# Loading the first tile of a split GELU-multiply with one transfer instead of two

## The chip, the cores and the metric

The kernel runs on one core of a Trainium2 chip. The metric is the device time of one execution in microseconds (us); less is better. Before the change the median of three runs is 469.26 us (469.21 to 469.45).

A core has computing engines with their own instruction streams (of these the kernel uses VectorE, called DVE in the profile, and ScalarE, called ACT), a SyncE (SP) that here only issues transfers, and 16 DMA engines that move the data between the device memory (HBM) and the on-chip buffers. Engines wait for each other and for transfers with semaphores.

## The reference

The input x is 32 x 512 x 2048 in float32. The last dimension is cut in two halves; the exact GELU of the first half is multiplied with the second.

```python
half_dim = x.shape[-1] // 2
x1, x2 = x[..., :half_dim], x[..., half_dim:]
gelu_x1 = 0.5 * x1 * (1 + erf(x1 / np.sqrt(2)))
return (gelu_x1 * x2).astype(np.float32)
```

The input has 134.22 MB and the output 67.11 MB. Every byte is read or written once.

## The kernel before

The 16384 rows are cut into 16 tiles of 1024 rows. A tile lies on 128 partitions, with R = 8 consecutive rows of 2048 numbers on each, so a partition's part of a tile is one contiguous stretch of 64 KB in HBM on the way in and 32 KB on the way out. There are two input buffers and two output buffers; tile i uses buffer k = i % 2 of each.

Everything is ordered by hand, with semaphores and three instruction streams:

- SP issues the loads (`load`, line 46) into queue q1. Loads 0 and 1 go out at the start (lines 60 to 64), load 0 in two halves: rows 0 to 3 of each partition with the semaphore `first[0]`, rows 4 to 7 with `first[1]`. Load i+2 goes out when the last multiplication of tile i is done (lines 107 to 109), since it overwrites the buffer that this reads.
- ACT computes the GELU (line 81) from the input buffer into the output buffer, and DVE multiplies it in place with the second half of the input rows (line 89). Both work in steps: rows 0 to 4 and 5 to 7 in most tiles; 0 to 1, 2 to 3 and 4 to 7 in tiles 0 and 15 (`pieces`, lines 72 and 73).
- ACT also issues the stores of tiles 0 to 13 (`store`, line 51) into queue q10. A store waits for the multiplication, and whatever comes next in ACT's program stands behind this wait. Tile 0 is stored in two halves of four rows, the first between ACT's second and third step. The store of tile 14 and the two half stores of tile 15 are issued by SP, into q1.

ACT begins a tile when its semaphore `ready[k]` has reached the count of everything issued on it so far (line 79). On `ready[k]` both the loads into buffer k and the stores from buffer k are counted, 16 each:

```python
            if i == 0 and lo % 4 == 0:
                nc.scalar.wait_ge(first[lo // 4], 16)
            elif lo == 0:
                nc.scalar.wait_ge(ready[k], n[ready[k].name])
```

So tile i (from 2 on) begins when both load i and store i-2 have landed; the second is needed because the GELU overwrites the output buffer. Only tile 0 waits for its two half loads apart, the second one ahead of the step of rows 4 to 7.

Of the kernel before, what the change touches and what calls it, by code (L numbers as in the profile page):

```python
# [1 line left out]

# [4 lines left out]

GELU = mybir.ActivationFunctionType.Gelu


@with_exitstack
def kernel(
    ctx: ExitStack,
    tc: tile.TileContext,
    x: bass.AP,
    out: bass.AP,
):
    nc = tc.nc
    P = nc.NUM_PARTITIONS

    x_flat = x.flatten_outer_dims()
    out_flat = out.flatten_outer_dims()
    n_rows, dim = x_flat.shape
    half = dim // 2

    R = 8
    x_t = x_flat.rearrange("(n p r) d -> n p r d", p=P, r=R)
    o_t = out_flat.rearrange("(n p r) d -> n p r d", p=P, r=R)
    n_tiles = x_t.shape[0]
    x_bufs = [nc.alloc_sbuf_tensor(f"x{k}_tile", [P, R, dim], x.dtype) for k in range(2)]  # L30
    o_bufs = [nc.alloc_sbuf_tensor(f"o{k}_tile", [P, R, half], out.dtype) for k in range(2)]

    first = [nc.alloc_semaphore(f"first{j}") for j in range(2)]
    ready = [nc.alloc_semaphore(f"ready{k}") for k in range(2)]
    gelu_done = nc.alloc_semaphore("gelu_done")
    mul_done = nc.alloc_semaphore("mul_done")
    tail_stored = nc.alloc_semaphore("tail_stored")
    n = {sem.name: 0 for sem in [*first, *ready, gelu_done, mul_done, tail_stored]}  # L40

    def counted(ins, sem, by):
        ins.then_inc(sem, by)
        n[sem.name] += by

    def load(i, rows, sem):
        ins = nc.sync.dma_start(out=x_bufs[i % 2][:, rows, :], in_=x_t[i][:, rows, :])  # L47
        counted(ins, sem, 16)
        return ins

    def store(queue, i, rows, sem):
        queue.wait_ge(mul_done, n[mul_done.name])
        counted(
            queue.dma_start(out=o_t[i][:, rows, :], in_=o_bufs[i % 2][:, rows, :]), sem, 16
        )

    for ins in (  # L60
        load(0, slice(0, 4), first[0]),
        load(0, slice(4, 8), first[1]),
        load(1, slice(0, 8), ready[1]),
    ):
        tc.no_tile_sem_insts.add(ins.ins.name)
    tc.close()
    tc.compile()  # L67

    for i in range(n_tiles):
        k = i % 2  # L70
        last = i == n_tiles - 1
        pieces = i == 0 or last
        steps = ((0, 2), (2, 4), (4, 8)) if pieces else ((0, 5), (5, 8))
        for lo, hi in steps:
            rows = slice(lo, hi)
            if i == 0 and lo % 4 == 0:
                nc.scalar.wait_ge(first[lo // 4], 16)
            elif lo == 0:
                nc.scalar.wait_ge(ready[k], n[ready[k].name])
            counted(  # L80
                nc.scalar.activation(  # L81
                    out=o_bufs[k][:, rows, :], in_=x_bufs[k][:, rows, :half], func=GELU
                ),
                gelu_done,
                1,
            )
            nc.vector.wait_ge(gelu_done, n[gelu_done.name])
            counted(
                nc.vector.tensor_mul(  # L89
                    out=o_bufs[k][:, rows, :],  # L90
                    in0=o_bufs[k][:, rows, :],
                    in1=x_bufs[k][:, rows, half:],
                ),
                mul_done,
                1,
            )
            if pieces and hi % 4 == 0:
                if last:
                    store(nc.sync, i, slice(hi - 4, hi), tail_stored)
                else:  # L100
                    store(nc.scalar, i, slice(hi - 4, hi), ready[k])
        if not pieces:
            if i == n_tiles - 2:
                store(nc.sync, i, slice(0, R), tail_stored)
            else:
                store(nc.scalar, i, slice(0, R), ready[k])
        if i + 2 < n_tiles:
            nc.sync.wait_ge(mul_done, n[mul_done.name])
            load(i + 2, slice(0, R), ready[k])


    nc.scalar.drain()  # L112
    for sem in (*first, *ready):
        nc.scalar.sem_clear(sem)
    nc.vector.drain()
    nc.vector.sem_clear(gelu_done)
    nc.sync.sem_clear(mul_done)
    nc.sync.wait_ge(tail_stored, n[tail_stored.name]).then_inc(
        tail_stored, -n[tail_stored.name]
    )  # L120


# [1 line left out]
_INS = ['x']  # L124
_OUTS = [((32, 512, 1024), 'float32')]


# [23 lines left out]
```

## Time and profile before

| | us |
|---|---|
| median of the runs | 469.26 |
| span of the profiled execution, first to last instruction | 467.9 |
| median less span | 1.4 |
| DVE busy, 34 multiplications | 140.5 |
| ACT busy, 35 instructions | 115.5 |
| DVE idle, waiting for ACT | 319.7 |
| ACT idle, waiting for stores | 301.6 |
| ACT idle, waiting for loads | 35.7 |
| one tile in the steady state (start of ACT to start of ACT) | 29.0 |

The page gives the span of the profiled execution and no total for it; what lies around the span is seen only by setting it beside the median of the runs.

How it is read: the page shows the busy time of each engine, the use of the DMA engines in 40 slices of 11.7 us, and the two queues with their packets, megabytes and share of the time of the 16 engines. The waits name the engine that waited, the tensor that it was going to write, and what released it ("<-"), with the sum, the number of times and the longest. The timeline has start, duration, engine, line, operation and shapes; "ACTq" and "SPq" are the issues of transfers. A transfer has landed when the instruction that waits for it starts.

Across the whole execution the 16 tiles' 134.22 MB were read and 67.11 MB written, 430 GB/s over the span.

### The profile page before, as it was taken

To read this page: it belongs to the slowest core of one execution; us is meant where nothing else is said; L and a number is where in the kernel's file an instruction comes from. 1 tells how busy PE (TensorE), PEld (TensorE's weight loads), DVE (VectorE), ACT (ScalarE), POOL (GpSimd) and SP (SyncE) were. 2 spreads that over 40 slices of the span, in tenths; PEclk is the share of its full clock that TensorE was granted. 3 is DMA by queue.
4 is the path that set the end of the run, shared out by engine and by line. 5 is a ranking of instruction groups with operands and counts; after the bars stand their busy time and mean duration, and the time that the engine had idled before them with its cause. 6 is when DMAs were issued, how large, how long until landed. Compare 5 with 4: busy or idle time off the path is not lost.

```text
span 467.9 us, 152 instructions
## 1 busy us (share of the span) xinstructions
DVE 140.5 (30%) x34; ACT 115.5 (25%) x35; POOL 0.2 (0%) x4
## 2 busy tenths in 40 slices
DVE  0330514207052060511606116060150702507043
ACT  1320606042060410604106050050500506014060
POOL 0000000000000000000000000000000000000000
DMA  8999999999999999999999999999999999999998
GB/s 359 448 448 443 403 405 492 409 403 448 459 437 403 434 417 493 403 403 448 476 420 403 445 406 493 403 406 445 487 409 403 445 451 448 403 434 417 493 389 373
DMA packets 5041, 201.34 MB, mean 430 GB/s; under 512 B 560, under 2 KB 560, under 8 KB 560
## 3 DMA queue, kind: packets, MB, share of 16 engines
q1 hardware_dynamic: 2880, 142.61, 70.6%
q10 hardware_dynamic: 2160, 58.72, 29.1%
q14 instruction: 1, 0.01, 0.0%
HBM read 134.22 MB, written 67.11 MB: 430 GB/s over the span
## 4 chain that ended last, share of the span: by engine, by line
DMA 76%; DVE 14%; ACT 8%; ACTq 0%; SPq 0%; issue 0%
DMA out_dram<-o_tile 66%; DVE o_tile L89 14%; DMA x_tile<-in_x_dram 10%; ACT o_tile L81 8%; ACTq L112 0%; SPq L47 0%
## 5 line engine op out<-in xcount | busy, mean ns | idle before, releaser
L89 DVE TENSOR_TENSOR o_tile<-o_tile,x_tile 128x5120 f32<-128x5120 f32 (+3 forms) x34 | 140.5, 4171 | 319.7 <-ACT o_tile L81 319.7
L81 ACT ACTIVATE o_tile<-x_tile 128x5120 f32<-128x5120 f32 (+3 forms) x34 | 114.3, 3407 | 337.4 <-DMA out_dram<-o_tile 301.6
L81 ACT ACT_TABLE_LOAD x1 | 1.3, 1283 | 2.9 <-PEq L67 2.9
L135 POOL MEMSET const-bfloat16-1.0<- 128x1 bf16 x1 | 0.1, 101 | 0.0
L135 POOL MEMSET const-uint8-127<- 128x1 uint8 x1 | 0.1, 101 | 0.0
L135 POOL MEMSET const-float32-0.0<- 128x1 f32 x1 | 0.1, 98 | 0.2 <-issue 0.2
L135 POOL MEMSET const-float32-1.0<- 128x1 f32 x1 | 0.1, 98 | 0.0
## 6 DMA issues: line engine op xcount, KB each, us to landing
out_dram<-o_tile ACTq DMA_DIRECT2D x13, 4096.0 KB, 44.7
x_tile<-in_x_dram SPq DMA_DIRECT2D x2, 4096.0 KB, 16.6
out_dram<-o_tile ACTq DMA_DIRECT2D x2, 2048.0 KB, 34.5
out_dram<-o_tile SPq DMA_DIRECT2D x1, 4096.0 KB, 25.2
out_dram<-o_tile SPq DMA_DIRECT2D x2, 2048.0 KB, 7.8
x_tile<-in_x_dram SPq DMA_DIRECT2D x15, 44.2
```

The costliest lines, as they stand in the source:

```text
L81: nc.scalar.activation(out=o_bufs[k][:, rows, :], in_=x_bufs[k][:, rows, :half], func=GELU),
L89: nc.vector.tensor_mul(out=o_bufs[k][:, rows, :], in0=o_bufs[k][:, rows, :], in1=x_bufs[k][:, rows, half:],),
L135: nc = _bacc.Bacc("TRN2", target_bir_lowering=False, num_devices=1)
```

## The change

The two half loads of tile 0 become one load of all eight rows of each partition. It is counted on `ready[0]`, like the later loads of that buffer; the two `first` semaphores go, and with them the wait ahead of rows 4 to 7 of tile 0. The steps of tile 0 (rows 0 to 1, 2 to 3, 4 to 7) and its two half stores stay as they are.

```diff
-    first = [nc.alloc_semaphore(f"first{j}") for j in range(2)]
     ready = [nc.alloc_semaphore(f"ready{k}") for k in range(2)]
@@
     for ins in (
-        load(0, slice(0, 4), first[0]),
-        load(0, slice(4, 8), first[1]),
+        load(0, slice(0, 8), ready[0]),
         load(1, slice(0, 8), ready[1]),
     ):
@@
-            if i == 0 and lo % 4 == 0:
-                nc.scalar.wait_ge(first[lo // 4], 16)
-            elif lo == 0:
+            if lo == 0:
                 nc.scalar.wait_ge(ready[k], n[ready[k].name])
@@
     nc.scalar.drain()
-    for sem in (*first, *ready):
+    for sem in ready:
         nc.scalar.sem_clear(sem)
```

The instructions of ACT and DVE are the same and in the same order; SP issues one transfer fewer.

More of the change, by code (lines that the diff above doesn't have):

```diff
@@ L39 @@
     tail_stored = nc.alloc_semaphore("tail_stored")
-    n = {sem.name: 0 for sem in [*first, *ready, gelu_done, mul_done, tail_stored]}
+    n = {sem.name: 0 for sem in [*ready, gelu_done, mul_done, tail_stored]}
     def counted(ins, sem, by):
```

## The prediction

> **What bounds the kernel now.** I read the page from the top: busy times, the DMA row of the 40 slices, the queues.
>
> ```profile
> span 467.9 us, 152 instructions
> DVE 140.5 (30%) x34; ACT 115.5 (25%) x35; POOL 0.2 (0%) x4
> DMA  8999999999999999999999999999999999999998
> q1 hardware_dynamic: 2880, 142.61, 70.6%
> q10 hardware_dynamic: 2160, 58.72, 29.1%
> ```
>
> The two computing engines are idle most of the time; the queues q1 (all loads and the last three stores, issued by SP) and q10 (the other stores, issued by ACT) keep the 16 DMA engines busy for 70.6 + 29.1 = 99.7% of the span. The kernel is bound by moving 201.34 MB. No order of transfers can gain much: only 0.3% (1.4 us) of the span is not DMA time, and the first packet is in the records only at 1.74 us, after a first issue at 0.73. What a change can do is to open a hole in the DMA.
>
> Then the waits, which show what a tile waits for, and the timeline of both ends.
>
> ```profile
> ACT o_tile L81 <- DMA out_dram<-o_tile: 301.6, 14, 21.9
> ACT o_tile L81 <- DMA x_tile<-in_x_dram: 35.7, 3, 21.1
> ```
>
> ```profile
> 12.76 3.71 ACT L81 ACTIVATE o_tile<-x_tile 128x2048 f32<-128x2048 f32 x2 [8.62 <-DMA x_tile<-in_x_dram]
> 19.23 0.38 ACTq L54 DMA_DIRECT2D out_dram<-o_tile  x1
> 22.46 3.62 ACT L81 ACTIVATE o_tile<-x_tile 128x4096 f32<-128x4096 f32 x1 [5.99 <-DMA x_tile<-in_x_dram]
> 30.57 0.36 ACTq L54 DMA_DIRECT2D out_dram<-o_tile  x1
> 47.20 7.12 ACT L81 ACTIVATE o_tile<-x_tile 128x5120 f32<-128x5120 f32 x2 [21.12 <-DMA x_tile<-in_x_dram]
> 71.57 7.12 ACT L81 ACTIVATE o_tile<-x_tile 128x5120 f32<-128x5120 f32 x2 [17.24 <-DMA out_dram<-o_tile]
> ...
> 432.86 27.74 SPq L54 DMA_DIRECT2D out_dram<-o_tile  x3
> 448.56 7.21 ACT L81 ACTIVATE o_tile<-x_tile 128x2048 f32<-128x2048 f32 x3 [21.87 <-DMA out_dram<-o_tile]
> ```
>
> Fourteen tiles (2 to 15) wait for a store, and not for their load alone: a buffer's semaphore counts the load of tile i+2 and the store of tile i together, and ACT waits for the sum. So a late store holds a tile whose data are there. How stores and loads share the engines stands in the DMA view, cut to the stretches 19 to 24.3, 24.3 to 46.3 and 46.7 to 71 us (packets, MB, share).
>
> ```profile
> q1 hardware_dynamic: 64, 2.10, 96.8%
> ...
> q1 hardware_dynamic: 113, 7.34, 77.4%
> q10 hardware_dynamic: 128, 2.10, 22.2%
> ...
> q1 hardware_dynamic: 144, 8.39, 79.7%
> q10 hardware_dynamic: 144, 2.10, 20.2%
> ```
>
> A transfer is 8 packets on each of 16 engines (one per partition) and a small one for the semaphore: 9 x 16 = 144. While both queues have work the engines take turns, one packet of each, whatever their sizes: in the last stretch all of load 2 (8.39 MB) went with all of the second half store (2.10 MB). The first stretch has no packet of q10, although the first half store was issued at 19.23. Its 64 packets of q1 are 16 semaphores and three data packets per engine; the store's first packet comes at 24.38, 5.15 us after its issue.
>
> Prices of a packet, from landings (starts of ACT). Load packet l (64 KB): half a load took 22.46 - 12.76 = 9.70, so l = 9.70/4 = 2.42. Load packet with a half-store packet (16 KB): 71.57 - 47.20 = 24.37, over 8 is 3.05. With a full store's packet s (32 KB): the next landing is at 100.56, 28.99 later, over 8 is 3.62; so s = 1.20 and the half-store packet is 0.63.
>
> **The change, part by part.**
>
> *One issue less on SP, two semaphores fewer.* SP issues load 1 about 0.43 us earlier (0.38 + 0.05 in the chain). It waits behind load 0 in the same queue until 21.6, so this gives nothing; were that cover gone it would be worth 0.43. At the end ACT clears two semaphores fewer, while SP still waits for the last store (7.2 us in its waits): nothing.
>
> *ACT starts at 22.46 and not at 12.76.* Load 0 has the same bytes on the same queue, so it lands when its second half did. The first half store is issued 19.23 - 12.76 = 6.47 later, at 28.93. ACT's last activation is queued behind it; its issue takes 0.38, and from there the activation, the multiplication and the issue take 30.57 - 22.46 = 8.11: the second half store (ACT) and load 2 (SP, waiting on the same multiplication) go out at 37.4 instead of 30.57. Neither makes the DMA idle: load 1 is queued and lasts past 41.
>
> *What is late next: the stores fall behind the loads.* Before, only one packet of load 1 went ahead of the first half store, so its 8 packets just fitted in with load 1's last seven (113 and 128 packets above), and since then a load and a store always ended together. Now load 1 runs alone from 21.6. If the store again needs 5.15 us, its first packet comes after 28.93 + 5.15 = 34.1, with 5 load packets gone (21.6 + 5 x 2.42 = 33.7). Of the half stores' 16 packets per engine, 4 get a turn before load 1 ends:
> - load 1 lands at 22.46 + 19.4 + 4 x 0.63 + 0.4 (the 0.4 is what the same sum leaves open before, 24.74 - 19.4 - 8 x 0.63 = 0.3, rounded up) = 44.8. Tile 1 takes 60.50 - 47.20 = 13.30 to its store's issue: 58.1 (before 60.50).
> - load 2 lands at 44.8 + 24.4 = 69.2, but 4 half-store packets are left, and tile 2 waits for them: 4 turns with load 3, 69.2 + 4 x 3.05 = 81.4 (before 71.57). Store 2 and load 4 are issued at 94.7 (before 84.86).
> - load 3 lands at 81.4 + 4 x 3.62 = 95.9; its last packet is some 1.0 us earlier, at 94.9. Load 4 needs about 1.0 from issue to first packet (the first load: 0.73 to 1.74), so 95.7: q1 is empty for a moment, and store 1, of which 4 packets are left, runs one or two alone. No DMA time is lost, and the lag shrinks to 3 packets (or 2).
> - With lag r, a load lands r x 1.20 earlier than before and its tile then waits r turns: net r x 2.42 later, 7.3 us for r = 3. Before, load i+2 was issued 15.7 us ahead of load i+1's landing (84.86 to 100.56), 14.7 ahead of its last packet. With lag r it is 14.7 - 3.62r: 3.8 for r = 3, enough against 1.0, and 0.2 for r = 4, not enough. So 3 is the largest lag that keeps itself, and nothing in the steady state (29.0 us per tile) takes it away.
>
> *The end.* Before, the SP queue carries store 14 and the two half stores of tile 15 without a hole: 8.39 MB from 448.56 to 467.9. With r store packets of tile 13 left when load 15 lands, these take turns with store 14's (1.20 each): load 15 lands 1.20r earlier, tile 15 is ready 1.20r later, 3.6 for r = 3. The half stores of tile 15 are issued that much later while the data ahead of them are gone on time, so the queue runs dry. The last half store was issued 27.4 after 432.86, at 460.23, and took 7.6 to land. Alone it would take 2.10 MB at the load rate, 4.85, plus what the first load needs beyond its bytes (12.76 - 0.73 - 9.70 = 2.33): 7.2. So 0.4 us of slack is there, at most 0.9, if the 0.5 us that the first packet of all took longer (1.71 against 1.21) isn't paid by a warm engine. Cost: 1.20r less 0.4 to 0.9, which is 2.7 to 3.2 for r = 3, 1.5 to 2.0 for r = 2, 0.3 to 0.8 for r = 1.
>
> I take r = 3 and 2.8, as the engines are warm at the end. The sum: 467.9 + 2.8 = 470.7 for the span. The page gives no total for its execution; the median of the runs, 469.26, is 1.4 above the span, and I add the same: 472.0 us.
>
> **A rule beside it.** The row first: in the stretch from 24.3 to 46.3 us 128 packets of the store stand among 113 of the load, single turns. The Trainium skill, "DMA: Bandwidth & Descriptors", section "Queues, rings and completion order", has an engine drain a whole packet of some 9 to 17 descriptors of one ring before it switches; a transfer here has 9 per engine, so a store would go as a block after one load. By that rule no store would fall behind by more than its own block, tiles would not wait for turns, and the sum would be 469.3. The row contradicts it, and I go by the row.
>
> **The rivals.**
> - *Not slower: the lag heals (469.3).* The wait of 5.15 us may not be a time but a number of packets already taken. Three per engine stand between the store's issue and its first packet. If three go first again, load packets 4, 5 and 6 (the fourth starts at 28.9), the store comes at 36.2 and only 3 of its packets run with load 1. Then 5 are left when load 2 has landed, load 4 is issued at 97.1, and load 3's last packet ends at 93.7; the 5 store packets of tile 1 need 6.0 us alone, to 99.7, and load 4 comes at about 98. They use the hole up, loads and stores are level again, and all is as before from tile 3 on. It decides if more than 5 load packets go first. For it: the count of three. Against it: 0.36 us stand empty ahead of that first store packet, as if it had just arrived, not long been taken.
> - *A lag of one (470.0).* If load 4's first packet needs nearer 2.5 us than 1.0, three store packets run alone: +0.3 to 0.8. Against it: the last half stores followed each other with no hole, the second 1.8 us after its issue.
> - *A lag of four or more, or holes in the middle (472.9 to 476).* Lag 4 kept costs 3.9 to 4.4. If the whole shift of tile 0 (37.4 - 30.57 = 6.9) came through, 476.2. Against that: full slices of the DMA everywhere.
> - *Faster.* Only the 0.43 us of the issue and the packets' overhead are to be had: 468.8 at best.
>
> **How the numbers follow.** No change is what lies within 0.2% (0.94 us) of 469.26. Lag 3: 0.42; lag 2 (471.0): 0.18; four or more: 0.07; lag 1: 0.07, nearly all within 0.2%; healed: 0.24; faster by over 0.2%: 0.02. Slower is 0.42 + 0.18 + 0.07 + 0.01 = 0.68, same 0.30, faster 0.02. The range takes in the healed case and lag 3 with its upper price: 469.0 to 473.0, which leaves out about 1 in 10. The likeliest case's own range, with lag 2, is 470.7 to 472.5.
>
> **What would show it.** Issues at 28.9 and 37.4; tile 1 starting at 44.8, before its old 47.20, tile 2 at 81.4, tile 3 at 108 and tile 4 at 137 (before 129.57), and then steps of 29 us with tiles 7 us late; the last tile starting at 452.2 and a slice under full DMA at the end. Tile 3 back at about 100 and the last tile at 448.6 would show the healed case. I am wrong if the engines don't take single turns while load 1 is under way, or if the lag drains in the steady state by a way that the trace of before can't show.

## The result, and the profile after

The changed kernel takes 474.13 us (median of four; 471.82 to 474.60) against 469.25 us before: ratio 1.0088, 95% interval 1.0069 to 1.0107. It is slower by 4.9 us, as forecast in sign, but above the range (469.0 to 473.0) and by nearly twice the 2.7 us forecast. Its times are 2.8 us apart, those of before 0.2 us. The profiled execution took 474.60, with a span of 473.2.

The page of the changed kernel: computing is as before, the queues have lost 0.5 and 0.3 points of share, and in the DMA row the fourth slice stands at 8 and the last but one at 7, where both stood at 9.

```profile
span 473.2 us, 149 instructions
DMA  8998999999999999999999999999999999999978
q1 hardware_dynamic: 2736, 142.61, 70.1%
q10 hardware_dynamic: 2160, 58.72, 28.8%
```

Its waits (engine, tensor, what released it; sum, times, longest):

```profile
ACT o_tile L77 <- DMA out_dram<-o_tile: 309.8, 14, 29.1
ACT o_tile L77 <- DMA x_tile<-in_x_dram: 31.3, 2, 19.1
```

Its timeline, cut to the start and the end:

```profile
22.73 3.71 ACT L77 ACTIVATE o_tile<-x_tile 128x2048 f32<-128x2048 f32 x2 [19.08 <-DMA x_tile<-in_x_dram]
...
29.20 0.38 ACTq L53 DMA_DIRECT2D out_dram<-o_tile  x1
...
37.73 0.36 ACTq L53 DMA_DIRECT2D out_dram<-o_tile  x1
45.45 7.12 ACT L77 ACTIVATE o_tile<-x_tile 128x5120 f32<-128x5120 f32 x2 [12.21 <-DMA x_tile<-in_x_dram]
...
81.72 7.12 ACT L77 ACTIVATE o_tile<-x_tile 128x5120 f32<-128x5120 f32 x2 [29.14 <-DMA out_dram<-o_tile]
...
105.90 7.12 ACT L77 ACTIVATE o_tile<-x_tile 128x5120 f32<-128x5120 f32 x2 [17.06 <-DMA out_dram<-o_tile]
...
134.85 7.12 ACT L77 ACTIVATE o_tile<-x_tile 128x5120 f32<-128x5120 f32 x2 [21.83 <-DMA out_dram<-o_tile]
...
426.90 7.12 ACT L77 ACTIVATE o_tile<-x_tile 128x5120 f32<-128x5120 f32 x2 [22.02 <-DMA out_dram<-o_tile]
...
440.19 26.83 SPq L53 DMA_DIRECT2D out_dram<-o_tile  x3
454.98 7.22 ACT L77 ACTIVATE o_tile<-x_tile 128x2048 f32<-128x2048 f32 x3 [20.96 <-DMA out_dram<-o_tile]
```

Tile 1 starts earlier than before (45.45 against 47.20), although tile 0 was late; tile 2 starts 10 us later (81.72 against 71.57), and the wait of 29.14 us ahead of it is for a store. Tile 4 is 5.3 us late (134.85 against 129.57), tile 14 7.3 (426.90 against 419.57), tile 15 6.4 (454.98 against 448.56). The end is only 5.3 us late: the last part, from tile 15's start to the end of the span, is 18.2 us where it was 19.3.

Where DMA time is lost at the end shows in the stretch from 457.9 to 462.2 us (columns: stretch and length; busy DVE, ACT, POOL; clock; DMA share; GB/s). First the changed kernel, then the one before:

```profile
457.90:462.20 4.30, 3.52 (x2) 4.30 (x2) 0.00 (x0) 1.00 0.14 61
```

```profile
457.90:462.20 4.30, 2.34 (x1) 0.00 (x0) 0.00 (x0) 1.00 1.02 436
```

Before, the DMA was full here; now it is 86% idle and waits for tile 15's first half store. By the row that is 3.7 us of empty DMA (the row counts a packet where it starts; by the packet records the engines stand empty for 3.6 us there).

One more place: the moment ahead of load 4, which was issued at 95.0. The DMA view of the changed kernel for 95.25 to 98.85 us, and then for 98.85 to 99.25:

```profile
q10 hardware_dynamic: 48, 1.57, 101.1%
q1 hardware_dynamic: 16, 0.00, 0.2%
```

```profile
q1 hardware_dynamic: 10, 0.66, 377.8%
q10 hardware_dynamic: 3, 0.10, 56.9%
```

In the first stretch the load queue has only semaphores: three store packets go alone on each of the 16 engines. Load 4 comes 3.9 us after its issue. In the second, ten engines start load 4 while three take one more store packet first (the other three start load 4 a moment later). From here on the engines are not at the same place. In what follows, engines are "in step" when they are at the same packet of a transfer at nearly the same time, and an engine "trails" when it ends its part of a transfer later than the others; a transfer has landed only when the last engine is done.

### The profile page after: what moved, and what is told of

Its sections match the earlier page's. It is cut to its first block, busy times and chain, and to the rows that moved or that the text cites. A ratio compares the mean times of both kernels' runs of the same rounds, so it can differ in the third digit from the quotient of the medians.

```text
span 473.2 us, 149 instructions
## 1 busy us (share of the span) xinstructions
DVE 140.5 (30%) x34; ACT 115.5 (24%) x35; POOL 0.2 (0%) x4
## 4 chain that ended last, share of the span: by engine, by line
DMA 76%; DVE 14%; ACT 8%; ACTq 0%; issue 0%; SPq 0%
DMA out_dram<-o_tile 67%; DVE o_tile L85 14%; DMA x_tile<-in_x_dram 9%; ACT o_tile L77 8%; ACTq L108 0%; SPq L46 0%
```

## The experiments

"Lag" is the number of turns by which the stores are behind the loads, counted where a load ends; a turn is one packet of each queue. The kernel before was measured beside each on the same chip, 469.26 to 469.34 us.

**Was it the late start or the one transfer?** Both half loads come back, but ACT waits for both at once:

```diff
-            if i == 0 and lo % 4 == 0:
-                nc.scalar.wait_ge(first[lo // 4], 16)
+            if i == 0 and lo == 0:
+                nc.scalar.wait_ge(first[0], 16)
+                nc.scalar.wait_ge(first[1], 16)
```

> The first tile is again loaded by two transfers of four rows, as before, but ACT waits for both ahead of its first step. Theory (the first stores are issued ten microseconds later, get their first turn after five load packets instead of one, and stay behind the loads from then on): nothing of this depends on the form of the load, so the time is that of the changed kernel, 471.8 to 474.6 us. Rival (the one large transfer itself, or its count on the shared semaphore, costs the time): 469.3 us.

472.68 us (472.20 to 472.94), ratio 1.0071 (1.0056 to 1.0086). Most of the loss, 3.3 of 4.9 us, is there with the old form of the load: what costs is that tile 0 begins when all of it has landed. The lower end of the changed kernel's times, not their middle, is met; whether the other 1.5 us belong to the form of the load or to how many engines trail is not shown. Its trace also shows something that was not expected: tile 2 starts at 83.89, load 4 comes later still, and by the packet records the stores catch up on fourteen of the 16 engines. Tile 4 is only 3.0 us late (132.58), but tiles 4 to 14 take 292.8 us. So most of the loss here is not a lag that all engines share: it comes from the two that did not catch up and trail.

**Is a late tile 0 enough?** The changed kernel with one store for tile 0, behind its last step:

```diff
-            if pieces and hi % 4 == 0:
-                if last:
-                    store(nc.sync, i, slice(hi - 4, hi), tail_stored)
-                else:
-                    store(nc.scalar, i, slice(hi - 4, hi), ready[k])
-        if not pieces:
+            if last and hi % 4 == 0:
+                store(nc.sync, i, slice(hi - 4, hi), tail_stored)
+        if not last:
```

> The changed kernel, but tile 0 is stored by one transfer of eight rows behind its last step, at about 34.5 us, so its data leave no earlier than in the changed kernel and the first store is issued 5 us later than there. Theory (what counts is the number of store packets that need a turn, 16 per engine for two half stores, 8 for one store): the store's 8 turns are done with load 2, no lag is left, tile 2 starts near 72 us and the time is 469.3 us (468.8 to 470.0). Rival (the late start of tile 0 is handed on to the end): 474 us or more, as the first store is later still.

470.14 us (469.93 to 470.47), ratio 1.0018 (1.0008 to 1.0027). The first store leaves 5 us later than in the changed kernel (34.23 against 29.20), and yet 4.0 of the 4.9 us are gone (474.13 - 470.14). Tile 2 starts at 74.55, not near 72. A late start does not hand itself on; what does is the number of store packets that still need a turn. By the packet records no store is behind here: when load 4 ends, two packets of the next store have already started. Tiles then wait for their loads, so tile 4 starts 3.1 us late (132.71), but the last loads have less left to share with, and the last step is 26.5 us instead of 29.0.

**And without a late start?** The kernel before, with tile 0's second half store cut into two of two rows:

```diff
-                    store(nc.scalar, i, slice(hi - 4, hi), ready[k])
+                    for r0, r1 in ((0, 4),) if hi == 4 else ((4, 6), (6, 8)):
+                        store(nc.scalar, i, slice(r0, r1), ready[k])
```

> The kernel before (two half loads, first activation at 12.8 us), but the second half store of tile 0 is cut into two of two rows. The bytes and the start are those of before. Theory (turns): tile 0 has 24 store packets per engine instead of 16, eight turns too many; tile 2 waits for the last of them until about 92 us (71.57 before), load 4 comes when the queue of the loads has long been empty, store 1 alone can't fill the hole and some 8 us of it stay: 476 to 479 us, and no lag is left afterwards. Rival (late start): tile 0 starts as before, so 469.3 us.

476.58 us (476.52 to 476.66), ratio 1.0155 (1.0140 to 1.0171): 7.2 us more for the same bytes in one more transfer, which is nine packets more per engine. Its timeline, tile 2 and tile 4:

```profile
91.13 7.12 ACT L81 ACTIVATE o_tile<-x_tile 128x5120 f32<-128x5120 f32 x2 [36.80 <-DMA out_dram<-o_tile]
...
137.00 7.12 ACT L81 ACTIVATE o_tile<-x_tile 128x5120 f32<-128x5120 f32 x2 [25.05 <-DMA out_dram<-o_tile]
```

and its DMA in the hole:

```profile
100.40:107.90 7.50, 3.99 (x2) 3.07 (x1) 0.00 (x0) 1.00 0.49 140
```

Tile 2 waits until 91.13 (92 expected) for store packets. Tile 4 is 7.4 us late and the span 7.3: all of it is lost by then and nothing afterwards. Most of it is the hole near 104 us. The row above counts a packet where it starts; by the packet records the engines stand empty for 5.6 us on the mean from 100 to 108 us, and the first packets of load 4 behind it last 1.25 us longer than 2.42 on the mean.

**The price of a lag, by itself.** The kernel before, early start kept, its second half store cut by partitions only, into three, four and five transfers (`store` is given a slice of partitions):

```diff
-                    store(nc.scalar, i, slice(hi - 4, hi), ready[k])
+                    cuts = (0, P) if hi == 4 else (0, 64, 96, 128)  # or (0, 32, 64, 96, 128), or (0, 32, 64, 96, 112, 128)
+                    for p0, p1 in zip(cuts, cuts[1:]):
+                        store(nc.scalar, i, slice(hi - 4, hi), ready[k], slice(p0, p1))
```

The same bytes in the same number of data packets; only small semaphore packets are added, one per engine and transfer.

> The kernel before, with the load in two halves and tile 0 as early as it was; only the second half store of tile 0 is cut by partitions into three transfers (64, 32 and 32 partitions, the same bytes). In the profile of the changed kernel a transfer's small semaphore packet takes a turn like a data packet, so this gives 8 + 3 = 11 turns where there were 9: a lag of two turns, made without any late start. With lag 2 load 4 is issued 14.7 - 7.2 = 7.5 us ahead of the end of load 3, so the queue of the loads never runs dry on the way. Theory: the lag stays to the end, tiles start some 4.8 us later than before in the steady state, and the tail costs 1.5 to 2.4 us: 470.8 to 471.7, with a narrow spread if the trailing engines come only from the queue running dry. Rival (the late start is what costs, or the lag drains): 469.3.

470.89 us (470.74 to 470.94), ratio 1.0033 (1.0020 to 1.0045).

> As the kernel with three pieces, but four (32 partitions each): 12 turns, a lag of three. Load 4 is issued 14.7 - 10.9 = 3.8 us ahead of the end of load 3; the changed kernel's load 4 needed 3.9 us from issue to its first packet, so this stands on the edge. Theory: 472.0 to 472.5 with a narrow spread if the queue does not run dry, else as the changed kernel, 471.8 to 474.6. Rival (the late start costs, or the lag drains): 469.3.

472.05 us (471.81 to 472.20), ratio 1.0058 (1.0043 to 1.0073).

> As the kernel with four pieces, but five (32, 32, 32, 16 and 16 partitions): 13 turns, a lag of four, which is what the changed kernel had when load 2 had landed. Theory: load 4 comes after the queue of the loads has run dry, store packets go alone, at different moments on different engines, and from there on all is as in the changed kernel: 471.8 to 474.6, engines out of step, wide spread. Rival (the late start costs): 469.3.

471.43 us (470.77 to 472.18), ratio 1.0046 (1.0031 to 1.0061). Two of its times are those of lag 2 and two those of lag 3, and its tile 4 starts at 137.16, three turns late: the fourth turn doesn't last, as expected (by the packet records fourteen engines are left with lag 2 and two with lag 3). But the wide loss of the changed kernel, expected with it, did not come: a miss.

Tiles 4, 14 and 15 with three transfers:

```profile
134.61 7.12 ACT L85 ACTIVATE o_tile<-x_tile 128x5120 f32<-128x5120 f32 x2 [21.83 <-DMA out_dram<-o_tile]
...
424.61 7.12 ACT L85 ACTIVATE o_tile<-x_tile 128x5120 f32<-128x5120 f32 x2 [21.83 <-DMA out_dram<-o_tile]
...
451.27 7.22 ACT L85 ACTIVATE o_tile<-x_tile 128x2048 f32<-128x2048 f32 x3 [19.54 <-DMA out_dram<-o_tile]
```

and with four:

```profile
136.97 7.12 ACT L85 ACTIVATE o_tile<-x_tile 128x5120 f32<-128x5120 f32 x2 [21.92 <-DMA out_dram<-o_tile]
...
426.98 7.12 ACT L85 ACTIVATE o_tile<-x_tile 128x5120 f32<-128x5120 f32 x2 [21.91 <-DMA out_dram<-o_tile]
...
452.36 7.22 ACT L85 ACTIVATE o_tile<-x_tile 128x2048 f32<-128x2048 f32 x3 [18.26 <-DMA out_dram<-o_tile]
```

Beside before (129.57, 419.57, 448.56) tile 4 is 5.0 and 7.4 us late, about 2.5 per turn; tiles 4 to 14 take 290.0 us in all three; the last step is 26.7 and 25.4 instead of 29.0, 1.20 less per turn. A lag of two or three neither grows nor drains under way.

**Is it paid in the tail?** Store 14 moved from SP's queue to that of the other stores; first in the changed kernel, then in the kernel with three transfers:

```diff
             if i == n_tiles - 2:
-                store(nc.sync, i, slice(0, R), tail_stored)
+                store(nc.scalar, i, slice(0, R), tail_stored)
```

> The changed kernel, but the store of tile 14 is issued by ACT into the queue of the other stores and not by SP behind the last load. Theory (the lag is paid at the end, where the two store packets of tile 13 that are left take turns with those of tile 14 and tile 15 starts late, so that the queue runs dry before its half stores): now the left packets go alone ahead of tile 14's, tile 15 starts 1.2 us earlier per packet of lag, 2.4 us for lag 2, and the hole of some 2.4 us closes: 469.3 us where the engines are in step, up to 472 where one engine trails as in the profile of the changed kernel. Rival (the time is lost on the way, not in the last tiles): as the changed kernel, 474 us.

476.20 us (472.89 to 477.93), ratio 1.0139 (1.0089 to 1.0189). A miss: no gain. In its profile tile 15 starts at 454.75, as late as in the changed kernel: it waits for trailing engines, and not for turns with store 14. Up to 440 us this is the changed kernel itself, so its trace is a second look at it: six engines, not three, took one store packet more ahead of load 4, and tiles 4 to 14 take 292.5 us.

> The kernel before with its second half store cut into three pieces (lag 2, engines in step, 470.89 us), and the store of tile 14 issued by ACT into the queue of the other stores. In the changed kernel this edit made things worse (476.2), with its engines out of step; here it meets the lag alone. Theory (a lag is paid only in the tail, where the left store packets of tile 13 take turns with store 14): they now go alone, tile 15 starts near 449.2 instead of 451.27, the DMA has no hole before the last half stores, and the time is 469.3 to 469.9. Rival (the 1.6 us are lost on the way, or in another place of the tail): 470.9.

469.64 us (469.50 to 470.53), ratio 1.0005 (0.9994 to 1.0017), not to be told from before. Its tile 15 and its DMA from 455 to 460 us:

```profile
448.56 7.21 ACT L85 ACTIVATE o_tile<-x_tile 128x2048 f32<-128x2048 f32 x3 [17.08 <-DMA out_dram<-o_tile]
```

```profile
455.00:460.00 5.00, 4.20 (x1) 0.77 (x1) 0.00 (x0) 1.00 1.00 428
```

and the same stretch with three transfers and store 14 in SP's queue:

```profile
455.00:460.00 5.00, 4.19 (x3) 3.49 (x1) 0.00 (x0) 1.00 0.86 367
```

With the engines in step a lag of two costs its 1.6 us nearly all in the tail: with the turns there gone the hole is closed, though tile 4 is still 4.8 us late (134.39).

**Fewer turns for a late tile 0.** The changed kernel with tile 0 stored as rows 0 to 3 of the first partitions, rows 4 to 7 of the same, and all rows of the other partitions:

```diff
-                    store(nc.scalar, i, slice(hi - 4, hi), ready[k])
+                    if hi == 4:
+                        store(nc.scalar, i, slice(0, 4), ready[k], slice(0, 48))    # second kernel: 64
+                    else:
+                        store(nc.scalar, i, slice(4, 8), ready[k], slice(0, 48))    # 64
+                        store(nc.scalar, i, slice(0, 8), ready[k], slice(48, P))    # 64
```

> The changed kernel with its one load, but tile 0 is stored in other pieces: rows 0 to 3 of partitions 0 to 47 (issued where the first half store was), then rows 4 to 7 of the same partitions, then all eight rows of partitions 48 to 127. That is 3 + 3 + 5 data packets and 3 semaphore packets per engine, 14 turns where the changed kernel has 18, so its lag of four turns should be gone although tile 0 is as late as there. Theory: tile 2 starts near 72 us, and the time is 469.3 to 470.2. Rival (the late start costs): 472 to 474.6.

472.40 us in the profiled execution. Its three other executions took 485.1 to 485.9 us; none of them has a trace, what made them 13 us longer is not known, and so no verdict is drawn from this kernel. Tile 2 starts at 73.21, so the fewer turns did bring it forward by 8.5 us, but the time is a miss: two engines trail by two to three microseconds from 75 us on.

> The changed kernel with its one load and its late tile 0, stored as rows 0 to 3 of partitions 0 to 63, then rows 4 to 7 of the same, then all rows of partitions 64 to 127: 4 + 4 + 4 data packets and 3 semaphore packets, 15 turns instead of 18. Of the five turns that the profile of the changed kernel shows open when load 2 has ended (four data packets and a semaphore), two should be left, so load 4 is issued some 7 us ahead of the end of load 3 and the queue of the loads never runs dry. Theory (the late start brings a lag; the rest, some 3 us, comes from the dry moment, in which engines pass from solo store packets to load 4 on different sides of a packet, fall out of step and trail): lag 2 without trailing engines, store 4 issued near 148, 471.0 to 471.9 with a narrow spread. Rival (the trailing engines come from the late start or the one load): 472 to 475, wide.

479.70 us (479.64 to 480.12), ratio 1.0222 (1.0205 to 1.0239): a clear miss. Tile 2 starts at 75.63, so load 4 came in good time and no queue was empty there, and still this kernel has the most trailing: tiles 4 to 14 take 295.8 us instead of 290.0. So an empty queue is not needed for engines to trail.

**A control for the one store.** The kernel before with the single store of tile 0 (the edit shown above for the changed kernel):

> The kernel before with its two half loads and early first activation, but tile 0 stored by one transfer of eight rows behind its last step (issued near 30.6 us): the control to the changed kernel with one store, which took 470.14. Theory (9 turns, no lag, DMA full): 469.2 to 470.2, tile 15 starting within 1 us of 448.6, narrow. Rival (the second half load's early landing is worth something of itself): at least 0.8 us faster than 470.14 and below the kernel before.

471.12 us (469.96 to 471.53), ratio 1.0032 (1.0022 to 1.0043). The rival is refuted: with one store the early start brings nothing. The number is missed by 0.9 us; tile 15 starts at 450.48, since one engine ends load 15 two microseconds behind the others. As with the other single store, the stores are ahead of the loads, here by two or three packets: tile 4 starts 5.5 us late (135.10), and the last step is 25.4 us.

**A common stop.** The changed kernel, both queues made empty once ahead of store 2 and load 4:

```diff
+        if i == 2:
+            for queue in (nc.scalar, nc.sync):
+                queue.wait_ge(ready[1], n[ready[1].name])
```

> The changed kernel, but ACT ahead of store 2 and SP ahead of load 4 also wait until load 3 and store 1 have landed, so that both queues are empty once, near 100 us. Three stores per tile-0 kernel had such a stop by itself and ran on in step (476.52 to 476.66). Theory (lag and trailing engines both come from queues joining under way; a common stop clears both): the stop costs about 2.4 us of empty DMA and the slower first packets 1 us, so 472.2 to 473.4, narrow, with tile 15 starting 19.3 us before the end of the span as before and not 18.2. Rival (engines fall out of step again for another reason): 474 or more, wide.

473.44 us (473.15 to 474.75), ratio 1.0086 (1.0057 to 1.0116), at the edge of what was expected, and less narrow. Tiles 4, 14 and 15:

```profile
133.55 7.12 ACT L77 ACTIVATE o_tile<-x_tile 128x5120 f32<-128x5120 f32 x2 [25.19 <-DMA out_dram<-o_tile]
...
423.54 7.12 ACT L77 ACTIVATE o_tile<-x_tile 128x5120 f32<-128x5120 f32 x2 [21.87 <-DMA out_dram<-o_tile]
...
452.56 7.21 ACT L77 ACTIVATE o_tile<-x_tile 128x2048 f32<-128x2048 f32 x3 [21.89 <-DMA out_dram<-o_tile]
```

Steps of 29.0 us to the last (290.0 and 29.0), and 19.2 us from there to the end: after the stop there is neither lag nor trailing. Only the stop is paid, 4.0 us at tile 4, so in time this comes out as dear as what it cures.

**Engines out of step on purpose.** The kernel before, second half store cut into pieces of which two run on half of the engines:

```diff
+                    cuts = (0, P) if hi == 4 else (0, 112, 120, 128)
```

> The kernel before, its second half store cut by partitions into 112, 8 and 8. The two small pieces run on half of the engines only, so these have 7 + 1 + 1 data and 3 semaphore packets, 12 turns, a lag of three, and the others 8 turns, one less than level: the engines are put out of step on purpose, with no late start and without a dry queue. Tiles wait for the engines with lag 3, and with all engines at lag 3 and in step the time was 472.05. Theory (engines out of step lose time of their own, as in the changed kernel): slow load packets, tiles more than 29.0 us apart, 473.5 or more. Rival (being out of step is harmless and the trailing engine of the changed kernel has another cause): 471.5 to 472.7, tiles 29.0 apart.

473.79 us (473.70 to 474.48), ratio 1.0095 (1.0078 to 1.0111). The number is the theory's, the mechanism is not. Tiles 4, 14 and 15:

```profile
139.22 7.12 ACT L85 ACTIVATE o_tile<-x_tile 128x5120 f32<-128x5120 f32 x2 [21.88 <-DMA out_dram<-o_tile]
...
429.38 7.12 ACT L85 ACTIVATE o_tile<-x_tile 128x5120 f32<-128x5120 f32 x2 [21.90 <-DMA out_dram<-o_tile]
...
454.82 7.21 ACT L85 ACTIVATE o_tile<-x_tile 128x2048 f32<-128x2048 f32 x3 [18.32 <-DMA out_dram<-o_tile]
```

Tile 4 is 9.7 us late, which is the price of four turns, and then every step is near 29.0 (290.2 in ten). Its packet records have no stretched load packet after 100 us (the changed kernel has 44, below). So engines out of step do cost, as the slowest one sets each tile, but for that reason alone they do not trail more and more.

## Why the prediction was right in sign and wrong in size

A table first; microseconds, from the starts of tiles 4, 14 and 15 and the spans:

| | tile 4 starts | tiles 4 to 14 | tile 14 to 15 | tile 15 to end | span |
|---|---|---|---|---|---|
| before | 129.57 | 290.0 | 29.0 | 19.3 | 467.9 |
| three transfers (lag 2) | 134.61 | 290.0 | 26.7 | 18.3 | 469.6 |
| four transfers (lag 3) | 136.97 | 290.0 | 25.4 | 18.3 | 470.7 |
| changed | 134.85 | 292.05 | 28.1 | 18.2 | 473.2 |

- **Bound by the DMA, and no gain to be had: right.** Nothing tried is faster than the kernel before; the nearest, at 469.64, can't be told from it.
- **The start: right, but one reading of the profile behind it was not.** Issues at 29.20 and 37.73 (28.93 and 37.4 said), tile 1 at 45.45 (44.8), tile 2 at 81.72 (81.4). The store's first packet stands in the records at 34.17, five load packets after the start of load 1 and 4.97 us after its issue. Of the two readings of the 5.15 us, a time or a count of three packets, the count does not hold: one or two load packets started on each engine between the store's issue and its first packet. So the healed case falls. What was said against it was wrong all the same: before the change no engine stood empty for 0.36 us ahead of the first store packet. The load packet there lasts 2.54 to 2.94 us instead of 2.42, and the store follows it at once. Rejecting the case was luck so far as it rested on that gap. Since a store's packet starts only where a load packet ends, the records fix the time from issue to being ready no better than between 2.8 and 5.0 us.
- **The lag that is left: nearly.** Said was 3, "or 2". Load 4 needed 3.9 us from issue to first packet, not the 1.0 of the first load on idle engines, so three store packets went alone, where one or two were said. By the packet records thirteen engines went from lag 4 to lag 2, and three to lag 1. The rule that 3 is the largest lag that lasts is borne out: lag 3 lasted (290.0 us for ten tiles), lag 4 fell back. Its margin was not as said: the 3.8 us that were reckoned for lag 3 stand against a need of 3.9, not of 1.0.
- **The price of a lag: right.** Said were 2.42 per turn in the start of tiles and, at the end, 1.5 to 2.0 us for lag 2 and 2.8 for lag 3. Measured in the span: 1.7 and 2.8. That it is paid in the tail is shown by the kernel with three transfers and store 14 in the other queue. From tile 15's start to the end it is 18.2 to 18.3 us in seven kernels whose engines, by the packet records, stood empty ahead of its half stores, the changed one among them; in two others (14 turns, and the changed kernel with store 14 in the other queue) it is 19.2 and 19.4, so this is no floor for all. One price was lower than the upper bound: in the changed kernel the two half stores of tile 15 took 6.8 and 6.4 us from issue to landing, not 7.2, and their packets last 0.61 to 0.65 us, with nothing of the longer first packet that was allowed for.
- **The step that failed: "nothing in the steady state (29.0 us per tile) takes it away".** It treats 16 engines as one and the step of 29.0 as given, so the sum has the tail's 2.8 us as its only cost and puts engines that trail at nothing, without a reason. (The sum as written also gives 472.1, not 472.0.) The span grew by 5.3 us. A lag of 2 with engines in step is worth 1.7 of it, less than the 2.8 for lag 3. Against that kernel the changed one loses 3.6 us more in the span: 0.2 up to tile 4, 2.05 from tile 4 to 14, 1.4 in the last step, and 0.1 less behind it. The packet records of its trace, put together to engines by the end of one packet and the start of the next, show how: after 100 us 44 load packets last 0.06 to 0.58 us longer than their 2.42 us, and all of them are on the three engines that took one more store packet ahead of load 4 (20 packets on one, 4.8 us in sum, and 24 on the other two, some 2.4 us on each). The other 13 engines have none, and neither has the kernel before. One of the three gets one per tile (at 190.9, 220.4, 249.9, 279.4, 308.9 and 338.3 us among others), falls back by some 0.4 us each time, and in the end every tile waits for it: the steps of tiles 10 to 14 are 29.1 to 29.7 us. The times of its executions lie apart, and the fastest, 471.82, is only 0.9 above what lag 2 costs in step (470.89); that it had less trailing is likely, but only one execution of this kernel has a trace.

What stretches those packets is open. The kernel that is the changed one up to 440 us has 108 of them after 100 us, 79 on the six engines that took one store packet more, but also 16 on an engine that took none more; so the split at load 4 does not settle alone which engines trail. The runs exclude the late start by itself (the changed kernel with one store has no such packet), the one transfer (with two half loads there are 22), the empty queue (with 15 turns load 4 came in time, and there are 326), and being out of step by itself (the uneven cut: none; the kernel before with one store, where one engine is two microseconds behind: none). That the split at load 4 starts it in the changed kernel fits both traces, and with the stop ahead of load 4 the slower steps are gone; but the stop clears more than that, so it is argued and not shown.

The Trainium skill, "DMA: Bandwidth & Descriptors", section "Anatomy of one DMA — SWDGE (gpsimd) path", calls the semaphore write at the end of a transfer on trn2 essentially free. It says so of transfers that GpSimd issues; those of this kernel are issued by SP and ACT. Here the packet lasts 9 ns, which agrees, but it takes a whole turn of its queue: two more of them, with no more data, cost 1.6 us (470.89 against 469.32).

## What to carry to other kernels

When DMA queues share engines packet by packet and something waits for both, count turns, not bytes: here two or three transfers more for the same bytes, or a first store later by four packets of the other queue, left one queue behind. Where that lag lasted to the end it was paid there (1.7 and 2.8 us of span); where it was far too large to last, it was paid at once, with empty engines (7.3 us with three stores). A kernel whose DMA is full can still be fragile: look at which queue stands ahead at each join, and at the tail's slack, before moving a first transfer. A model with all engines in step gave too little here (1.7 of 5.3 us). A spread in the times of one kernel can be a sign that they are not in step (2.8 us in the changed kernel), but the lack of one says nothing: the kernel that trails most lies within 0.5 us.

## What the runs showed of the hardware that was not expected

- A transfer's 9 ns semaphore packet takes a turn: with two and three transfers more for the same data packets tile 4 starts 5.0 and 7.4 us late.
- From issue to first packet 1.0 us on idle engines, but 5.0 for the first half store (which had to wait for a load packet's end) and 3.9 for load 4, with the other queue at work. The load packet that runs ahead of the first store packet is longer than the others, 2.54 to 2.94 us against 2.42 in the kernel before.
- Engines take up a queue that was empty at packet borders of their own, so one issue can put them out of step: ten against three in the stretch shown above. After both queues were empty at once they ran in step (tiles 29.0 us apart to the last).
- On some engines out of step load packets last up to 0.58 us longer in the changed kernel, with the cause unknown; half of the 44 stand right behind the engine's own store semaphore.
